# Making the split parts of queries and keys over 128 rows and moving them with transfers inside SBUF

## Chip, cores and metric

The kernel runs on one core of a Trainium2 chip. The metric is the device time of one execution in microseconds (us). The kernel before takes 1759.96 us, the median of 3 runs (1759.52 to 1761.84).

## What is computed

The input is one sequence of 512 rows with 1024 columns in float32. Four parts follow one another: a differential attention with a gated feed-forward net, a chunked attention with a relative-position bias and another such net, a block that mixes two other mechanisms, and a last feed-forward net. Only the two attentions matter here. Cut to the lines that the change touches:

```python
# differential attention, 8 heads, each with two maps m of 64 columns
q = apply_rope(q, cos, sin) * (A_HEAD_DIM ** -0.5)
k = apply_rope(k, cos, sin)
sc = einsum('bqhmd,bkhmd->bhmqk', q, k)          # chunk-causal mask, then softmax over k
a = p[:, :, 0] - lam * p[:, :, 1]
o = einsum('bhqk,bkhe->bqhe', a, v)
...
# chunked attention, 16 heads of 64 columns
sc = einsum('bnqhd,bnkhd->bhnqk', q, k_band) + bias
o = einsum('bhnqk,bnkhd->bnqhd', softmax(sc), v_band)
```

## The kernel before, in words

**Precision by parts.** TensorE multiplies in a reduced float32 form (F32R). To keep the precision, an operand w is split into a high part hi (a copy into F32R, on ScalarE) and a low part lo = w - hi (on VectorE), and a product is the sum of three: hi*hi, hi*lo, lo*hi (`passes`, L293 to L296). Weights come from HBM over the SP queue (`Weights.load`, L65), are split at L126 and L129, and are then used.

**Queries and keys.** A projection makes 128 rows by 512 columns, transposed: 64 rows for each of two maps of one head (differential attention) or for two heads (chunked attention). The product of scores for one of the two needs only 64 rows, so `stacked` (L556) stacks high and low parts to fill 128. For queries, tile `qk` 0 or 1 holds the high part in the map's own 64 rows and the low part in the other 64. For keys, `qk` 2 or 3 holds the high part in both halves, and `kl` the low part in both. Two products then give all four terms (`stacked_scores`, L580): L581 with the high keys, L582 with the low keys. `stacked` makes each 64-row piece by an instruction of its own: L569 copies the own high part, L571 makes the low part, for keys L573 copies the high part to the other rows and L578 (differential attention) or L575 (chunked, `twice=True`) makes the low part for the other rows. ScalarE and VectorE may write other rows than they read.

**Differential attention** (`attention_a`, L585). After a projection, `rope` (L621) turns the rows: four ScalarE copies (L626) into x[3], then three VectorE operations (L627 to L629) with a result in gb[:, 0]. Three steps of the projection stream later (`DELAY`), `rope_split` calls `stacked` on it. `scores` (L657) makes, for a block of 128 queries, the two maps' scores, their maxima (L670), exponentials with sums (L671, `accum_out`), a copy of the first map's sum into `sums[h]` (L677), and the combination (L676 to L680). `transposes` (L684) brings the result to the rows that `values_product` (L695) needs; `norm_sums` and `norm_apply` follow, with a power on POOL (L717).

**Chunked attention** (`attention_b`, L825). `split` calls `stacked` on the projection's bank in PSUM. `load_bias` (L833) loads 128 x 512 biases of one head through POOL's queue into one of `BB` = 3 buffers and then sets a corner with a POOL memset (L837). `scores` adds the bias with L873, which frees the buffer when its last block is done.

**Order.** `run_slots` (L343) goes through slots. Each slot has parts, four slots per head (`later(4 * h + n, scores, ...)`, transposes two slots later, and so on), and a stream of projection steps is paid out between them by a cost of 1.3 per step and a rate per slot: `A_RATE` = (3.4, 29, 2.0), `B_RATE` = (2.0, 54, 1.25). In the first attention the projection of a head completes some slots ahead of its first scores, in the second further ahead. Outside `manual_schedule` blocks (and but for SP, whose order is the program's everywhere) the Tile scheduler decides each engine's order when the program is built, from priorities, data and its own estimates of durations; on the chip each engine's queue runs in that fixed order. `qk` and `kl` have two buffers each, so the parts of a head wait for the scores of the head two before. The same two `qk` buffers take split weights at the end of an attention.

Of the kernel before, what the change touches and what calls it, by code (L numbers as in the profile page):

```python
# [10 lines left out]
F32 = mybir.dt.float32  # L11
F32R = mybir.dt.float32r
AF = mybir.ActivationFunctionType
OP = mybir.AluOpType
# [4 lines left out]
S, D = 512, 1024  # L19
NT = S // 128  # L20
# [14 lines left out]

DELAY = 3

BB = 3


WO2, AT = (4, 4, 0, 0), ((0, 4), (0, 4), (0, 2))
# [125 lines left out]
def body(ctx, tc, ins, out, stop=None, dbg=None):  # L167
    nc = tc.nc
# [78 lines left out]
    small = ctx.enter_context(tc.tile_pool(name="small", bufs=4))  # L247
# [7 lines left out]
    x = [const.tile([128, D], F32, name=f"x{t}") for t in range(NT)]  # L255
# [29 lines left out]
    gb = const.tile([128, 2, D], F32, name="gb")  # L285
# [12 lines left out]
    def bank(*shape):  # L298
        return psum.tile([128, *(shape or (512,))], F32, name="ps")
# [253 lines left out]
                stream += [(1.3, lambda g=n - 8, t=t, c=c: values(g, t, c)) for t in range(NT) for c in range(2)]  # L553
        return stream

    def stacked(pool, qk, j, which, p, scale=0.125, twice=False):  # L556

        if which == 0:
            both = pool.tile([128, 4 * S], F32, name="qk").bitcast(F32R)
            qk[j] = [both[:, n * S:n * S + S] for n in range(4)]
            kl = pool.tile([128, 2 * S], F32, name="kl").bitcast(F32R)
            qk[j] += [kl[:, :S], kl[:, S:]]
        part, rows, sc = qk[j], (slice(0, 64), slice(64, 128)), scale if which == 0 else 1.0
        for m in range(2):
            own, other, src, st = rows[m], rows[1 - m], p[rows[m]], part[2 * which + m]
            nc.scalar.activation(st[own], src, AF.Copy, scale=sc)  # L569
            lo = st[other] if which == 0 else part[4 + m][own]  # L570
            nc.vector.scalar_tensor_tensor(lo, src, sc, st[own].bitcast(F32), op0=OP.mult, op1=OP.subtract)  # L571
            if which == 1:
                nc.scalar.activation(st[other], src, AF.Copy)  # L573
                if twice:
                    nc.vector.scalar_tensor_tensor(part[4 + m][other], src, sc, st[own].bitcast(F32),  # L575
                                                   op0=OP.mult, op1=OP.subtract)
                else:
                    nc.scalar.activation(part[4 + m][other], lo.bitcast(F32), AF.Copy)  # L578

    def stacked_scores(p, part, m, i, N):  # L580
        yield lambda: nc.tensor.matmul(p[:, :N], part[m][:, ts(i)], part[2 + m][:, :N], start=True, stop=False)  # L581
        yield lambda: nc.tensor.matmul(p[:, :N], part[m][:, ts(i)], part[4 + m][:, :N], start=False, stop=True)  # L582


    def attention_a(es, oT, wo):  # L585
        pool = lambda name, bufs, **kw: es.enter_context(tc.tile_pool(name=name, bufs=bufs, **kw))
        persist, work = pool("a_const", 1), pool("a_work", 2)
# [3 lines left out]
        gcol, lam = cols_a[:, 0:1], cols_a[:, 4:8]  # L591
# [20 lines left out]
        qk, V, state, late = {}, {}, {}, []  # L612
# [17 lines left out]
            late.append([DELAY, rope_split, (h, which, r)])  # L630

        def rope_split(h, which, r):
            stacked(work, qk, h, which, r)

        def project(h, which, part):
            tick(1)
# [18 lines left out]
        soft, sums = {}, {}  # L655

        def scores(h, i, place):  # L657
            n = 128 * (i + 1)
            N = max(256, n)
            st = small.tile([128, 8], F32, name="a_st")  # L660

            e = x[(4 * h + place) % 3].rearrange("p (m k) -> p m k", m=2)
            ps = [bank(), bank()]
            for products in zip(*(stacked_scores(ps[m], qk[h], m, i, N) for m in range(2))):
                for product in products:
                    product()
            for m in range(2):
                p = ps[m]
                nc.vector.memset(p[0:64, n - 64:n], NEG)
                nc.vector.tensor_reduce(st[:, m:m + 1], p[:, :n], axis=AX.X, op=OP.max, negate=True)  # L670
                nc.scalar.activation(e[:, m, :n], p[:, :n], AF.Exp, bias=st[:, m:m + 1],  # L671
                                     accum_out=st[:, 2 + m:3 + m])

            if h not in sums:
                sums[h] = small.tile([128, NT], F32, name="a_s0")
            nc.vector.reciprocal(st[:, 4:5], st[:, 3:4])  # L676
            nc.vector.tensor_copy(sums[h][:, i:i + 1], st[:, 2:3])  # L677
            nc.vector.scalar_tensor_tensor(st[:, 5:6], st[:, 4:5], lam[:, 3:4], st[:, 2:3],
                                           op0=OP.mult, op1=OP.mult)
            nc.vector.scalar_tensor_tensor(e[:, 0, :n], e[:, 1, :n], st[:, 5:6], e[:, 0, :n],  # L680
                                           op0=OP.mult, op1=OP.add)
            soft[h, i] = e
# [142 lines left out]
    def attention_b(es, oT, wo, tails):  # L825
        pool = lambda name, bufs, **kw: es.enter_context(tc.tile_pool(name=name, bufs=bufs, **kw))
        persist, work = pool("b_const", 1), pool("b_work", 2)
        aT = tuple(persist.tile([128, 4, S], F32R, name=f"aT{q}") for q in "hl")
        for a in aT:
            nc.vector.memset(a[:, 3, 256:384].bitcast(F32), 0.0)  # L830
        qk, V, bias, soft, state, o_ = {}, {}, {}, {}, {}, {}

        def load_bias(hd):  # L833
            t = work.tile([128, S], F32, name="bias", bufs=BB)
# [3 lines left out]
            bias[hd] = t  # L838

        def split(j, which, p):  # L840
            stacked(work, qk, j, which, p, -0.125, True)

        def project(j, which, part):
            p = part_project(("bq" if which == 0 else "bk", j), state, part)
# [517 lines left out]
```

## Time and profile before

| what | value |
|---|---|
| time, median of 3 runs | 1759.96 us (1759.52 to 1761.84) |
| the profiled execution's own time | 1759.88 us |
| its span, first to last instruction | 1758.0 us |
| TensorE (PE) busy | 1727.9 us, 98% |
| VectorE (DVE) busy | 1184.7 us, 67% |
| ScalarE (ACT) busy | 875.1 us, 50% |
| GpSimd (POOL) busy | 70.9 us, 4% |
| granted TensorE clock, mean | 0.998 |
| differential attention | about 20 to 240 us |
| chunked attention | about 620 to 840 us |

The busy share is a mean over all stages. Matmuls are pipelined and their ends are modelled, so a busy TensorE need not be at its peak. Who waited for whom is inferred from semaphores; idle time of an engine that does not limit costs nothing by itself.

### The profile page before, as it was taken

The numbers are of one execution on the slowest core, as the hardware profiler recorded it, in microseconds if no ns is written. First come the engines' busy times: TensorE is split into PE (matmuls) and PEld (weight loads), VectorE is DVE, ScalarE is ACT, GpSimd is POOL, SyncE is SP. The second block draws the span as 40 slices with busy tenths as digits, with TensorE's granted clock in tenths as the row PEclk, the third lists the DMA queues.
The fourth block names the chain that finished last, engine by engine and source line by source line (L and its number), as shares of the span: only waits on it lengthen the run. The fifth ranks groups of instructions, "written<-read, shape, count | busy, mean of one in ns | idle before, by whom it ended". The sixth has DMA issues, their size and how long they took to land.

```text
span 1758.0 us, 26549 instructions
## 1 busy us (share of the span) xinstructions
PE 1727.9 (98%) x10496; PEld 1527.2 (87%) x10496; DVE 1184.7 (67%) x2028; ACT 875.1 (50%) x1470; POOL 70.9 (4%) x125
## 2 busy tenths in 40 slices
PE   8899999999999999999999999999999999999998
PEld 8688879999988888888899999888877899988886
DVE  6888856988844567767689888347546588763333
ACT  6878833444533258888344444333425445552221
POOL 0000002000000000000000000001001100000000
PEclk9999999999999999999999999999999999999999
DMA  6221226333443142322324244341322233443321
GB/s 206 61 61 61 83 97 206 108 110 107 120 132 120 48 120 79 97 78 73 108 78 118 84 131 139 102 121 49 109 73 91 72 86 96 128 124 108 97 96 48
DMA packets 198235, 176.83 MB, mean 101 GB/s; under 512 B 7008, under 2 KB 175136, under 8 KB 198112
## 3 DMA queue, kind: packets, MB, share of 16 engines
q1 hardware_dynamic: 194384, 162.48, 30.9%
q0 software_dynamic: 3152, 10.84, 2.1%
q8 instruction: 82, 1.34, 0.3%
q10 hardware_dynamic: 576, 1.84, 0.3%
q14 instruction: 41, 0.34, 0.1%
HBM read 172.99 MB, written 7.38 MB: 103 GB/s over the span
## 4 chain that ended last, share of the span: by engine, by line
PE 89%; ACT 6%; DVE 4%; issue 1%; DMA 0%; POOL 0%; SPq 0%; DVEq 0%; POOLq 0%; ACTq 0%
PE ps L296 52%; PE ps L382 30%; PE ps L896 1%; PE ps L312 1%; PE ps L884 1%; ACT whi L126 1%; ACT x L626 1%; PE ps L581 1%; PE ps L582 1%; ACT qk L573 1%; DVE wlo L129 1%; ACT qk L569 0%; PE ps L688 0%; ACT b_e L875 0%; PE ps L1096 0%
## 5 line engine op out<-in xcount | busy, mean ns | idle before, releaser
L126 ACT ACTIVATE whi<-wraw 128x1024 fp32r<-128x1024 f32 (+2 forms) x326 | 329.3, 1014 | 310.1 <-PE ps L296 183.7
L129 DVE TENSOR_TENSOR wlo<-wraw,whi 128x1024 fp32r<-128x1024 f32 (+2 forms) x326 | 379.9, 1168 | 133.9 <-ACT whi L126 132.2
L296 PE MATMUL ps<-xh,whi 128*128 128x256 f32 (+1 forms) x1260 | 406.6, 324 | 1.0 <-ACT xh L314 1.0
L296 PE MATMUL ps<-xl,whi 128*128 128x256 f32 (+1 forms) x1260 | 405.4, 322 | 0.5 <-DVE xl L315 0.3
L296 PE MATMUL ps<-xh,wlo 128*128 128x256 f32 (+1 forms) x1260 | 405.6, 322 | 0.0
L296 PEld LDWEIGHTS ps<-xh,whi 128*128 128x128 f32 x1260 | 238.5, 190 | 18.7 <-ACT xh L314 2.4
L296 PEld LDWEIGHTS ps<-xh,wlo 128*128 128x128 f32 x1260 | 239.4, 190 | 17.1
L296 PEld LDWEIGHTS ps<-xl,whi 128*128 128x128 f32 x1260 | 239.5, 190 | 16.9 <-DVE xl L315 1.0
L382 PE MATMUL ps<-whi,sh 128*128 128x512 f32 x568 | 175.9, 390 | 0.0
L382 PE MATMUL ps<-wlo,sh 128*128 128x512 f32 x568 | 175.5, 389 | 0.0
L382 PE MATMUL ps<-whi,sl 128*128 128x512 f32 x568 | 175.5, 389 | 0.0
L296 PE MATMUL ps<-th,whi 128*128 128x256 f32 x624 | 173.2, 277 | 0.0
L296 PE MATMUL ps<-tl,whi 128*128 128x256 f32 x624 | 172.8, 277 | 0.0
L296 PE MATMUL ps<-th,wlo 128*128 128x256 f32 x624 | 172.6, 277 | 0.0
L764 DVE TENSOR_TENSOR sl<-h,sh 128x512 fp32r<-128x512 f32 x76 | 52.1, 690 | 177.1 <-ACT sh L763 177.1
L763 ACT ACTIVATE sh<-h 128x512 fp32r<-128x512 f32 x76 | 46.7, 629 | 212.9 <-PE ps L382 204.1
L382 PEld LDWEIGHTS ps<-wlo,sh 128*128 128x128 f32 x568 | 106.6, 188 | 22.2
L382 PEld LDWEIGHTS ps<-whi,sl 128*128 128x128 f32 x568 | 106.6, 188 | 22.2
L382 PEld LDWEIGHTS ps<-whi,sh 128*128 128x128 f32 x568 | 106.3, 188 | 21.8
L296 PE MATMUL ps<-whi,xh 128*128 128x256 f32 (+1 forms) x384 | 125.1, 326 | 0.0
L296 PE MATMUL ps<-wlo,xh 128*128 128x256 f32 (+1 forms) x384 | 123.1, 321 | 0.0
L296 PE MATMUL ps<-whi,xl 128*128 128x256 f32 (+1 forms) x384 | 123.1, 321 | 0.0
(333 smaller groups left out, 2840.9 us busy)
## 6 DMA issues: line engine op xcount, KB each, us to landing
wraw<-in_ffn_w_in SPq DMA_DIRECT2D x76, 512.0 KB, 4.4
wraw<-in_w_ff SPq DMA_DIRECT2D x61, 512.0 KB, 4.0
wraw<-in_ffn_w_out SPq DMA_DIRECT2D x44, 512.0 KB, 3.6
wraw<-in_a_w_qkv SPq DMA_DIRECT2D x23, 512.0 KB, 3.9
wraw<-in_w_in SPq DMA_DIRECT2D x20, 512.0 KB, 3.8
wraw<-in_kv_w SPq DMA_DIRECT2D x16, 512.0 KB, 4.0
room<-in_ffn_w_in SPq DMA_DIRECT2D x12, 512.0 KB, 4.0
copies<-extd POOLq DMA_DIRECT2D x16, 320.0 KB, 8.2
```

What stands on the lines that cost most here:

```text
L126: self.nc.scalar.activation(hi[:, sl], t[:, sl], AF.Copy)
L129: self.nc.vector.tensor_tensor(lo[:, sl], t[:, sl], hi[:, sl].bitcast(F32), op=OP.subtract)
L296: nc.tensor.matmul(ps, lhs[a][lsel], rhs[b][rsel], start=first and n == 0, stop=last and n == 2)
L312: nc.tensor.transpose(p[:, k, :], y[:, ts(4 * c + k)], ident)
L382: nc.tensor.matmul(self.banks[t][c], act[a][:, ts(t)], w[b][:, 0, c * 512:(c + 1) * 512], start=first and n == 0, stop=last and n == 2)
L573: nc.scalar.activation(st[other], src, AF.Copy)
L581: yield lambda: nc.tensor.matmul(p[:, :N], part[m][:, ts(i)], part[2 + m][:, :N], start=True, stop=False)
L582: yield lambda: nc.tensor.matmul(p[:, :N], part[m][:, ts(i)], part[4 + m][:, :N], start=False, stop=True)
L626: nc.scalar.activation(qs[32 * g:32 * g + 32], p[32 * (g ^ 1):32 * (g ^ 1) + 32], AF.Copy)
L763: nc.scalar.activation(hi, src[k], AF.Copy)
L764: nc.vector.tensor_tensor(lo, src[k], hi.bitcast(F32), op=OP.subtract)
L884: nc.tensor.transpose(p[:, j], e[:, ts(j)], ident)
```

## The change

`stacked` gets two scratch tiles of 128 rows, `hi` and `lo`. One ScalarE copy makes the high part of all 128 rows and one VectorE operation the low part. Then transfers inside SBUF, issued on POOL's queue, bring 64 rows at a time to their places: four for queries, eight for keys. The variant `twice` is gone. In the differential attention the scratch is a half of x[3] (the rope's work rows) for hi and the rope's result itself for lo, a half each for queries and keys. In the chunked attention it is a half of gb[:, 0] and a new tile `low`, the same for queries and keys; `BB` goes from 3 to 2. In `scores` of the differential attention the exponential's sum of the first map goes straight into `sums[h]`, so the copy L677 is gone, and `sums[h]` is allocated ahead of the products.

```diff
-BB = 3
+BB = 2
...
-    def stacked(pool, qk, j, which, p, scale=0.125, twice=False):
+    def stacked(pool, qk, j, which, p, hi, lo, scale=0.125):
...
+        hi, lo, move = hi.bitcast(F32R), lo.bitcast(F32R), nc.gpsimd.dma_start
+        nc.scalar.activation(hi, p, AF.Copy, scale=sc)
+        nc.vector.scalar_tensor_tensor(lo, p, sc, hi.bitcast(F32), op0=OP.mult, op1=OP.subtract)
         for m in range(2):
-            own, other, src, st = rows[m], rows[1 - m], p[rows[m]], part[2 * which + m]
-            nc.scalar.activation(st[own], src, AF.Copy, scale=sc)
-            lo = st[other] if which == 0 else part[4 + m][own]
-            nc.vector.scalar_tensor_tensor(lo, src, sc, st[own].bitcast(F32), op0=OP.mult, op1=OP.subtract)
-            if which == 1:
-                nc.scalar.activation(st[other], src, AF.Copy)
-                if twice:
-                    nc.vector.scalar_tensor_tensor(part[4 + m][other], src, sc, st[own].bitcast(F32),
-                                                   op0=OP.mult, op1=OP.subtract)
-                else:
-                    nc.scalar.activation(part[4 + m][other], lo.bitcast(F32), AF.Copy)
+            own, other = rows[m], rows[1 - m]
+            if which == 0:
+                move(part[m][own], hi[own])
+                move(part[m][other], lo[own])
+            else:
+                for r in rows:
+                    move(part[2 + m][r], hi[own])
+                for r in rows:
+                    move(part[4 + m][r], lo[own])
...
-            stacked(work, qk, h, which, r)
+            stacked(work, qk, h, which, r, x[3][:, which * S:which * S + S], r)
...
+            if h not in sums:
+                sums[h] = small.tile([128, NT], F32, name="a_s0")
             for products in zip(*(stacked_scores(ps[m], qk[h], m, i, N) for m in range(2))):
...
                 nc.scalar.activation(e[:, m, :n], p[:, :n], AF.Exp, bias=st[:, m:m + 1],
-                                     accum_out=st[:, 2 + m:3 + m])
-
-            if h not in sums:
-                sums[h] = small.tile([128, NT], F32, name="a_s0")
+                                     accum_out=st[:, 3:4] if m else sums[h][:, i:i + 1])
             nc.vector.reciprocal(st[:, 4:5], st[:, 3:4])
-            nc.vector.tensor_copy(sums[h][:, i:i + 1], st[:, 2:3])
-            nc.vector.scalar_tensor_tensor(st[:, 5:6], st[:, 4:5], lam[:, 3:4], st[:, 2:3],
+            nc.vector.scalar_tensor_tensor(st[:, 5:6], st[:, 4:5], lam[:, 3:4], sums[h][:, i:i + 1],
...
+        low = persist.tile([128, S], F32, name="low")
...
-            stacked(work, qk, j, which, p, -0.125, True)
+            stacked(work, qk, j, which, p, gb[:, 0, S:], low, -0.125)
```

## Rows read from the trace of the kernel before

**Rows 1.** Stretches of both attentions: length, busy us (instructions), clock, DMA share, GB/s.
```profile
core 0: us, PE busy (x) PEld busy (x) DVE busy (x) ACT busy (x) POOL busy (x), PEclk, DMA share, GB/s
40.00:240.00 200.00, 188.10 (x1089) 161.30 (x1088) 162.41 (x420) 155.44 (x325) 8.58 (x8) 0.99 0.24 74
640.00:840.00 200.00, 197.26 (x1133) 167.72 (x1132) 144.88 (x363) 161.51 (x364) 8.89 (x26) 1.00 0.29 85
```
**Rows 2.** TensorE's waits in 40 to 245 us: total, times, longest.
```profile
PE ps L688 <- DVE a_s L677: 2.9, 1, 2.9
PE ps L296 <- ACT aTh L690: 2.1, 2, 1.7
PE ps L688 <- DVE x L680: 2.1, 1, 2.1
PE ps L581 <- ACT qk L573: 1.5, 2, 1.2
```
**Rows 3.** Stretches of 2 us behind the wait at 86 us; columns as in group 1.
```profile
86.00:88.00 2.00, 1.22 (x6) 1.25 (x7) 1.97 (x6) 1.95 (x4) 0.00 (x0) 0.62 0.00 0
88.00:90.00 2.00, 2.00 (x11) 2.00 (x11) 1.94 (x4) 1.97 (x4) 0.00 (x0) 0.52 0.00 0
```
**Rows 4.** Instructions that write tile qk: ns min/median/max, first and last start.
```profile
L569 ACT ACTIVATE qk<-gb x32: 615/628/635, 29.7 to 201.9; 64x512 fp32r<-64x512 f32 x32
...
L569 ACT ACTIVATE qk<-ps x32: 573/592/596, 633.6 to 795.8; 64x512 fp32r<-64x512 f32 x32
L571 DVE SCALAR_TENSOR_TENSOR qk<-gb,qk x16: 685/686/689, 32.1 to 193.3; 64x512 fp32r<-64x512 f32 x16
L573 ACT ACTIVATE qk<-gb x16: 628/630/632, 32.8 to 203.2; 64x512 fp32r<-64x512 f32 x16
...
L573 ACT ACTIVATE qk<-ps x16: 574/589/597, 640.1 to 797.6; 64x512 fp32r<-64x512 f32 x16
```
**Rows 5.** Instructions that write tile kl.
```profile
L571 DVE SCALAR_TENSOR_TENSOR kl<-gb,qk x16: 673/686/690, 34.0 to 202.6; 64x512 fp32r<-64x512 f32 x16
L578 ACT ACTIVATE kl<-kl x16: 615/629/632, 34.8 to 204.4; 64x512 fp32r<-64x512 f32 x16
L571 DVE SCALAR_TENSOR_TENSOR kl<-ps,qk x16: 664/689/695, 638.5 to 796.4; 64x512 fp32r<-64x512 f32 x16
L575 DVE SCALAR_TENSOR_TENSOR kl<-ps,qk x16: 683/689/694, 641.4 to 798.4; 64x512 fp32r<-64x512 f32 x16
```
**Rows 6.** Lines L677 and L706.
```profile
L677 DVE COPY a_s<-a_st x32: 132/144/156, 41.9 to 224.4; 128x1 f32<-128x1 f32 x32
...
L706 ACT ACTIVATE gb<-a_o x8: 629/632/635, 77.8 to 232.2; 128x512 f32<-128x512 f32 x8
```
**Rows 7.** Tile bias: issue (ns), its engine's idle time (us, times), landing.
```profile
L835 POOL DMA_DIRECT2D bias<-copies x16: 536/536/612, 615.9 to 803.8; - x16
...
  DVE b_st L873: 62.9, 7
  DMA bias<-copies: 41.7, 16
...
DMA to landing us min/median/max: 2.8/3.3/6.1
```
**Rows 8.** DMA issues by line: KB each, median us to landing.
```profile
extd<-gb POOLq DMA_DIRECT2D x1, 15.9 KB, 1.6
```
**Rows 9.** Timeline of POOL, near 280 us: start, us, line, operation.
```profile
279.79 4.16 POOL L822 DMA_DIRECT2D copies<-extd  x8 [1.68 <-DMA extd<-gb]
```
**Rows 10.** Pieces of the chain of waits in order of time: start us, us, what.
```profile
55.32 0.60 DVE gb L629
...
60.14 0.64 ACT kl L578
...
132.04 0.63 ACT kl L578
...
179.10 0.61 DVE gb L629
...
184.74 0.63 ACT kl L578
```
**Rows 11.** Timeline of VectorE at 128 us.
```profile
127.91 0.68 DVE L629 TENSOR_TENSOR gb<-gb,x 128x512 f32<-128x512 f32 x1
```

## The prediction, made before the changed kernel ran

> **What bounds the kernel now.** I read the busy shares first, then the two attention stages by stretches, then who TensorE waits for, and last the pieces of the chain of waits. TensorE is busy for 98% of the span, so the change, which takes no product away, can give back only time in which TensorE stands still. In the differential attention (40 to 240 us) TensorE is busy for 188.1 of 200 us beside ScalarE's 155 and VectorE's 162; in the chunked attention (640 to 840 us) for 197.3 of 200 [rows 1]. That leaves 11.9 and 2.7 us, a floor, since the ends of matmuls are modelled. What the reader is to see in the waits is that none is for a weight load: transposes, value products and scores wait for ScalarE and VectorE, whose queues run late [rows 2]. One such wait costs twice: after the 2.9 us one TensorE ran at a granted clock of 0.62 and then 0.52 for four microseconds, its 1.2 GHz level [rows 3]. Of its busy 1.22 and 2.00 us there, 0.38 and 0.48 are lost, 1.4 us in all. So the most that can come back is about 11.9 + 2.7 + 1.4 = 16 us.
>
> The profiled execution took 1759.88 us with a span of 1758.0; the median of the runs shown is 1759.96, the same within 0.1. I work from 1759.9.
>
> **What is removed.** In the first attention, per head, two ScalarE copies for the queries and six for the keys, and two VectorE subtractions for each: 32 x 0.628 + 16 x 0.630 [rows 4] + 16 x 0.629 [rows 5] = 40.2 us of ScalarE, and 32 x 0.686 = 22.0 us of VectorE [rows 4, 5]. In the second, 32 x 0.592 + 16 x 0.589 = 28.4 us of ScalarE [rows 4], and 32 of L571 and 16 of L575 at 0.689 = 33.1 us of VectorE [rows 5]. The copy of sums is 32 x 0.144 = 4.6 us of VectorE [rows 6]. The order of `sums[h]` before the products is no instruction; it costs nothing.
>
> **What is added.** Per stage 16 copies and 16 subtractions over 128 rows. A copy of twice the rows takes no longer: the 128x512 one from SBUF took 0.632 us [rows 6], the 128x512 VectorE operation 0.68 [rows 11]. So ScalarE pays back 16 x 0.63 = 10.1 us in the first stage and 16 x 0.59 = 9.4 in the second, VectorE 16 x 0.69 = 11.0 in each. Net: first stage ScalarE -30.1, VectorE -15.6 us (19% and 10% of their busy time); second stage -19.0 and -22.1 (12% and 15%).
>
> Then 12 transfers per head or pair, 96 per stage, of 64 rows x 2 KB = 128 KB, all on POOL's queue. An issue there took 0.536 us [rows 7], and eight went out back to back in 4.16 us [rows 9], so 12 are 6.4 us of a queue that does almost nothing else: per stage 51 of 200 us beside 9. The bytes are 96 x 0.128 = 12.6 MB in 200 us, 63 GB/s more beside 74 and 85, at a DMA share of 0.24 and 0.29 [rows 1]; even doubled it is not full, and no weight is waited for, so I put the loads at nothing. If that cover were gone, a weight's split would wait on ScalarE, and TensorE for it.
>
> **The unknown: how long a transfer takes to land.** No row shows one from SBUF to SBUF. Below stands 1.6 us for 15.9 KB [rows 8], above 6.1 us, the worst of the 256 KB bias loads, three of which went out together; their median was 3.3 [rows 7]. I take 3.3, since half the bytes is offset by eight in a row. The keys are complete 0.63 (the high part) + 8 x 0.54 (the issues; the subtraction runs beside the first two) + 3.3 = 8.2 us after the rope's last addition; with the two ends 6.6 and 11.0. Today it takes from the end of L629 to the end of the last L578: 60.8 - 55.9 = 4.9 us, 132.7 - 128.6 = 4.1 and 185.4 - 179.7 = 5.7 [rows 10, 11]; a fourth head near 200 us has 4.9. So the keys become later by 3.3, 4.1, 2.5 and 3.3 us.
>
> **Where later keys matter.** By the slots and rates the projection stream leaves heads 0, 2, 3 and 5 most of a slot or more (a slot is 5 to 6 us) between the split and the first score, and heads 1, 4, 6 and 7 (the four above) next to nothing: TensorE already waits there for L573 [rows 2]. In the second stage the stream is ahead by three slots or more from the second pair on; only the first pair is tight.
>
> **What the path gets.** First stage: the 2.9 us wait at 86 us hangs on a norm chain behind ScalarE's L569 and L573; it loses some 2 us and the 1.4 of the clock, 3.4 together. The 2.1 us for x (L680, near 139 us) comes after six key copies, 3.9 us of ScalarE that shrink to 0.6: all 2.1. The 2.1 us for L690 hangs on one copy and four rope copies: 1.2. The smaller ones, half of 3: 1.5. Sum 8.2 us. The waits for L573 stay, as waits for a transfer. Second stage: 1.2 of 2.7, its waits being softmax latencies that only a shorter queue helps. New waits: between nothing and 13.2 us (the four heads' whole delay). The scheduler places the scores by its own estimate of the transfers and fills TensorE from the projection stream, so I take the low side, 2.0 us, the first pair of the second stage included. The sum is -8.2 - 1.2 + 2.0 = -7.4: **1752.5 us**.
>
> What moves to POOL brings its waits along. A bias load there waits for the last score of an earlier head (62.9 us over seven), and the memset behind each load waits for its landing (41.7 us over 16) [rows 7]; transfers queued behind these wait too, 3 us or so. `BB = 2` moves the load from two heads ahead to one; four slots of some 3 us cover 0.5 + 3.3 + 0.1 us: nothing, unless twelve issues stand ahead of it (6.4 us), and then it still arrives. The scratch rows (x[3], gb, low) are written again a projection later, 5 slots of the stream, 7 us: just after 8.2 us of transfers begin to clear, so ScalarE could be held for a microsecond; in the range.
>
> A POOL issue beside busy VectorE shows no lengthening here: minimum and median are both 0.536 us, with VectorE 72% busy [rows 1, 7]. The Trainium skill, "SBUF — State Buffer", section "SBUF: two separate sides", warns of the contrary: descriptors of a transfer issued from GpSimd are held while VectorE runs certain copies through both ports. By that rule every issue could wait out one VectorE instruction; by the row none does.
>
> **Rivals.**
> - *The tight heads wait in full (slower).* If the order on TensorE stays as today, the four heads' scores stand at the front for 13.2 us instead of 2.0, and two of the waits of over 3 us lower the clock again (1.4 each, about 3): 1752.5 + 11 + 3 = 1766. It decides once the transfers land more than about 2 us later than the scores are placed. For it: TensorE waits at this place now. Against it: a planner that sees the transfers. 0.16.
> - *POOL's issues stretch.* Each of eight issues held for one VectorE instruction of 0.69 us makes the keys 5.5 us later; on four heads, with half of it filled by other products, +11 and 3 of clock: 1767. The 16 issues at 0.536 us speak against it. It is the rule of the Trainium skill named above. 0.03.
> - *A draw.* Half of the 8.2 comes back, because the chains behind the waits (softmax, rope's four copies) are untouched, and the new waits take 4: 1759.9 - 4.1 - 0.6 + 4 = 1759. 0.18.
> - *Nearly all idle time goes.* ScalarE at 125 of 200 us catches up, and the new waits are filled: -14 of the 16: 1746. 0.13.
> - *The forecast*: 0.50, its own range 1747 to 1757. That the copies or subtractions would not be halved is excluded by the code.
>
> **Numbers.** About 0.2%, 3.5 us, can be told from no change. Faster takes 0.13 + most of 0.50: 0.60; within 0.2% the draw's larger part and the forecast's end: 0.17; slower 0.23. The range 1744 to 1765 takes in all but the far ends of the slow cases.
>
> **What would show it.** Right: L569 to L578 gone from ScalarE, 32 operations of 0.63 and 0.69 in their place; TensorE idle in 40 to 240 us down from 11.9 to about 6; no wait for VectorE near 86 and 139 us, no clock below 0.9 there; POOL busy some 60 us per stage, landings near 3 us. Wrong: L581 waiting for transfers on heads 1, 4, 6 and 7 with several microseconds each; ScalarE waiting for transfers before L626 or the high part; POOL's queue filled by waits; new idle time of TensorE elsewhere from another order.

## The result, and the profile after

The changed kernel took 1782.24 us (median of 4 runs, 1777.99 to 1783.17) beside 1760.39 of the kernel before on the same chip: ratio 1.0118, 95% interval 1.0102 to 1.0134. It is 21.9 us slower; the forecast was 7.4 faster. The profiled execution took 1783.17 us with a span of 1781.4, against 1758.0 before: 23.4 us to be found.

First where they lie. Three marks of the trace cut the span: the last product of the output weights with tile oT of the first attention, the first copy of a high part in the second, and the last output-weight product there.

```
us                                    before    after   difference
start to last oT product, first       267.5     275.0    +7.5
from there to the second attention    366.1     366.2    +0.1
first copy to last oT product, second 231.8     242.5   +10.7
from there to the end                 892.6     897.7    +5.1
```

Each attention lost, although ScalarE and VectorE got their relief. The stretches of [rows 1], after the change (length, busy us and instructions of PE, PEld, DVE, ACT, POOL, granted clock, DMA share, GB/s):

```profile
40.00:240.00 200.00, 183.11 (x1053) 157.89 (x1053) 147.13 (x371) 129.56 (x282) 50.38 (x91) 0.97 0.52 125
640.00:840.00 200.00, 188.94 (x1098) 162.66 (x1098) 114.98 (x302) 135.45 (x303) 59.04 (x124) 0.98 0.66 149
```

ScalarE is down from 155 and 162 to 130 and 135 us, and TensorE stands still for 16.9 and 11.1 us where it did for 11.9 and 2.7. The DMA share has doubled. The lines that replaced [rows 4, 5], first attention and then second (busy, mean ns of one, idle time of the engine before them and what ended it):

```profile
L569 ACT ACTIVATE x<-gb 128x512 fp32r<-128x512 f32 x16 | 10.1, 629 | 12.3 <-DVE gb L631 11.0 <-DVE a_st L678 1.2
L570 DVE SCALAR_TENSOR_TENSOR gb<-gb,x 128x512 fp32r<-128x512 f32 x16 | 10.8, 678 | 0.4 <-ACT x L569 0.3
...
L569 ACT ACTIVATE gb<-ps 128x512 fp32r<-128x512 f32 x16 | 9.5, 591 | 10.9 <-DMA qk<-gb 10.8
L570 DVE SCALAR_TENSOR_TENSOR low<-ps,gb 128x512 fp32r<-128x512 f32 x16 | 11.0, 686 | 17.8 <-DMA qk<-low 11.1 <-DMA kl<-low 3.8 <-ACT gb L569 2.9
```

The durations are those forecast. What is new is at the end of the lower two: in the second attention both engines wait for transfers before they may write the scratch rows again.

TensorE's waits in 40 to 245 us answer to [rows 2] (total, times, longest):

```profile
PE ps L584 <- DMA kl<-gb: 8.5, 4, 4.1
PE ps L583 <- DMA qk<-x: 3.9, 2, 3.1
PE ps L583 <- DMA kl<-gb: 2.7, 2, 1.4
PE ps L689 <- DVE x L681: 1.2, 2, 1.0
```

The waits at 86 and near 139 us for the softmax chain are gone but for 1.2 us, and so is the clock's fall of [rows 3] (1.00 from 86 to 90 us). In their place stand 15.1 us of waits for transfers, at heads 0, 1, 4 and 6. Two of them bring the clock down in their turn: after 2.5 us at head 0 it stood at 0.67 and 0.50 from 46 to 50 us, and at head 6, after waits of 3.1 and 4.1 us, it was back at 1.2 GHz until near 197 us. Stretches of 2 us at head 6, columns as above:

```profile
186.00:188.00 2.00, 0.00 (x0) 0.00 (x0) 1.83 (x3) 0.04 (x1) 0.63 (x2) 0.66 1.04 148
188.00:190.00 2.00, 0.00 (x0) 0.00 (x0) 0.00 (x0) 0.58 (x1) 0.51 (x1) 0.50 1.13 309
190.00:192.00 2.00, 1.11 (x2) 0.63 (x3) 1.05 (x3) 0.00 (x0) 0.06 (x1) 0.50 0.68 129
```

TensorE did nothing for four microseconds and came back at 0.50, its 1.2 GHz level. In the second attention the same view (630 to 890 us) names a wait of 4.5 us for a transfer, at the first scores, one more of 0.5 us, and softmax waits, which have grown. After the change, then before it:

```profile
PE ps L583 <- DMA qk<-gb: 4.5, 1, 4.5
PE ps L886 <- ACT gb L879: 3.9, 4, 1.5
PE ps L886 <- ACT b_e L879: 2.2, 3, 1.5
```
```profile
PE ps L884 <- ACT b_e L877: 1.1, 3, 0.7
PE ps L884 <- ACT gb L877: 0.5, 3, 0.2
```

The transfers into tile kl, first and second attention (issue: ns min/median/max, first and last; then issue to landing, us):

```profile
L580 POOL DMA_DIRECT2D kl<-gb x32: 509/542/578, 35.8 to 214.0; - x32
DMA to landing us min/median/max: 2.5/3.4/7.2
...
L580 POOL DMA_DIRECT2D kl<-low x32: 509/537/569, 650.6 to 818.4; - x32
DMA to landing us min/median/max: 2.2/5.0/8.3
```

The issue is as forecast (0.536), the landing 3.4 us in the middle of the first attention, but 5.0 in that of the second, and 7.2 and 8.3 at worst. Last, the end: the instructions of the kernel's last line on POOL's queue, before and after.

```profile
L1358 POOLq DRAIN  x3: 51/98/4175, 1752.3 to 1757.8; - x3
```
```profile
L1360 POOLq DRAIN  x3: 51/97/9973, 1770.6 to 1781.1; - x3
```

Before the program ends, POOL's queue is drained; that took 4.2 us and now 10.0, while SP and the compute engines stand finished. This is the +5.1: of the 5.8 us that the drain grew by, the rest passed while the last output was still on its way.

### The profile page after: what moved, and what is told of

The parts are those of the page before. It is cut to its first block, busy times and chain, and to the rows that moved or that the text cites. A ratio compares the mean times of both kernels' runs of the same rounds, so it can differ in the third digit from the quotient of the medians.

```text
span 1781.4 us, 26859 instructions
## 1 busy us (share of the span) xinstructions
PE 1732.6 (97%) x10496; PEld 1531.9 (86%) x10496; DVE 1145.6 (64%) x1948; ACT 829.8 (47%) x1390; POOL 169.4 (10%) x317
## 4 chain that ended last, share of the span: by engine, by line
PE 54%; DMA 2%; issue 1%; DVE 1%; ACT 1%; POOL 0%; DVEq 0%; POOLq 0%; ACTq 0%
PE ps L296 30%; PE ps L382 21%; DMA qk<-low 1%; PE ps L898 1%; PE ps L886 1%; PE ps L312 0%; PE ps L1098 0%; DMA qk<-gb 0%; PE ps L1103 0%; PE ps L583 0%; DMA kl<-low 0%; PE ps L584 0%; DVE wlo L129 0%; PE ps L1062 0%; PE ps L1116 0%
## 5 line engine op out<-in xcount | busy, mean ns | idle before, releaser
L382 PEld LDWEIGHTS ps<-whi,sh 128*128 128x128 f32 x568 | 106.3, 188 | 21.7
```

Of the source, the lines that this page charges most:

```text
L382: nc.tensor.matmul(self.banks[t][c], act[a][:, ts(t)], w[b][:, 0, c * 512:(c + 1) * 512], start=first and n == 0, stop=last and n == 2)
```

## The experiments

The theory (T): the transfers take more than the relief gives, by their landing in front of the scores, by the scratch rows that they hold, and by POOL's closing drain. Rivals: another order of TensorE's products (O); a relief worth nothing (L). Thirteen more kernels ran. In the table, "first" and "second" are the two attentions by the marks above, "rest" the stretch to the end, and the count is of the transfers that POOL issues in the whole program.

```
                              median  ratio to before, interval   first  second  rest   POOL count, drain
before                        1760.4  1                           267.5  231.8   892.6   43   4.17
changed                       1782.2  1.0118 (1.0102 to 1.0134)   275.0  242.5   897.7  235   9.97
transfers left out            1742.7  0.9901 (0.9887 to 0.9915)   253.9  228.2   892.8   43   4.17
new way in first alone        1766.4  1.0037 (1.0025 to 1.0048)   271.3  231.8   892.8  139   2.13
new way in second alone       1774.1  1.0081 (1.0068 to 1.0095)   268.1  243.3   892.4  139   2.13
before, 192 idle transfers    1769.6  1.0053 (1.0039 to 1.0067)   271.9  231.8   898.0  235   9.97
DELAY = 1                     1778.7  1.0105 (1.0090 to 1.0120)   268.8  244.6   897.7  235   9.97
transfers on SP               1760.6  1.0000 (0.9990 to 1.0009)   262.6  238.8   893.0   43   4.17
own halves direct             1759.6  0.9997 (0.9987 to 1.0006)   260.7  235.3   897.1  107   9.40
tight heads the old way       1762.8  1.0015 (1.0005 to 1.0024)   264.6  238.2   892.3  163   4.09
own halves, SP                1757.9  0.9984 (0.9976 to 0.9993)   262.7  235.8   892.8   43   4.17
own halves, SP, pair 0 old    1751.8  0.9953 (0.9940 to 0.9967)   260.3  230.6   892.5   43   4.17
own halves, 32 idle more      1755.4  0.9971 (0.9960 to 0.9983)   260.9  234.2   892.4  139   2.13
before, sums edit alone       1761.8  1.0006 (0.9997 to 1.0015)   269.5  231.8   892.6   43   4.17
tight old, B queries old      1754.2  0.9962 (0.9949 to 0.9976)   263.5  230.2   892.3  135   1.81
```

The stage lengths are of one profiled execution each; runs of one kernel differ by up to 6.5 us (the changed one's by 5.2), so differences of 1 or 2 us between rows are not read as effects.

### Transfers left out

```diff
-        nc.scalar.activation(hi, p, AF.Copy, scale=sc)
-        nc.vector.scalar_tensor_tensor(lo, p, sc, hi.bitcast(F32), op0=OP.mult, op1=OP.subtract)
-        for m in range(2):
-...
+        nc.scalar.activation(part[2 * which], p, AF.Copy, scale=sc)
+        nc.vector.scalar_tensor_tensor(part[4 if which else 1], p, sc, part[2 * which].bitcast(F32),
+                                       op0=OP.mult, op1=OP.subtract)
...
-        yield lambda: nc.tensor.matmul(p[:, :N], part[m][:, ts(i)], part[2 + m][:, :N], start=True, stop=False)
-        yield lambda: nc.tensor.matmul(p[:, :N], part[m][:, ts(i)], part[4 + m][:, :N], start=False, stop=True)
+        yield lambda: nc.tensor.matmul(p[:, :N], part[m][:, ts(i)], part[2][:, :N], start=True, stop=False)
+        yield lambda: nc.tensor.matmul(p[:, :N], part[m][:, ts(i)], part[4][:, :N], start=False, stop=True)
```

> The changed kernel with its 192 transfers left out: the high and the low part are written once over 128 rows, straight into the tiles that the score products read, so the two halves are not brought to their rows (the scores are therefore not those of the reference), and scratch rows are not used. Theory T (the transfers are the loss: their landing at the tight heads, the scratch rows they hold, and POOL's closing drain): with them gone the relief stands alone, about 1745 to 1757 us, below the kernel before; the waits for POOL's tiles qk and kl before the scores vanish, and the closing drain is back from 10.0 to about 4.2 us. Rival O (another order on TensorE and new softmax waits make the loss, with or without transfers): 1765 us or more. Rival L (transfers cost, but the relief is worth nothing): 1758 to 1762.

1742.65 us, a little below the range of T: the relief alone is worth 17.9 us, and the transfers cost 1782.24 - 1742.65 = 39.6. O and L fall. In this kernel both maps of a head read the same two key tiles; the number and the shapes of the products are as before. TensorE's stretches and its only waits of 40 to 245 us that are left:

```profile
40.00:240.00 200.00, 198.03 (x1151) 172.12 (x1150) 157.89 (x395) 132.73 (x291) 9.63 (x10) 1.00 0.26 81
640.00:840.00 200.00, 199.82 (x1146) 170.87 (x1145) 126.06 (x340) 140.31 (x326) 10.48 (x29) 1.00 0.27 81
```
```profile
PE ps L296 <- ACT aTh L680: 0.9, 1, 0.9
PE ps L713 <- POOL a_r L707: 0.6, 1, 0.6
PE ps L382 <- DVE oTl L717: 0.2, 1, 0.2
PE ps L678 <- DVE x L670: 0.2, 1, 0.2
```

Idle time falls from 11.9 to 2.0 and from 2.7 to 0.2 us. By the table the relief is 13.6 us in the first attention and 3.6 in the second; the transfers then take 21.1, 14.3 and 4.9 us in the two attentions and at the end.

### One attention at a time

The first edit is that of the new way in the first attention alone (with three bias buffers and without low), the second that of the second alone.
```diff
-            stacked(work, qk, j, which, p, gb[:, 0, S:], low, -0.125)
+            stacked_old(work, qk, j, which, p, -0.125, True)
...
-            stacked(work, qk, h, which, r, x[3][:, which * S:which * S + S], r)
+            stacked_old(work, qk, h, which, r)
```

> The new way in the first (differential) attention alone; the second goes as in the kernel before (three bias buffers, no extra scratch). By the matmul-by-matmul comparison of the two traces the first attention lost 7.5 us, the second 10.8 and the end 5.1 (96 of 192 issues would be 2.6 of it). Theory T, losses add up stage by stage: 1760.4 + 7.5 + 2.6 = about 1770.5 (1768 to 1773). Rival: the second stage's loss comes from what the first left (shifted order, DMA): then 1778 or more. Rival: the first stage's loss is an accident of its order that goes with the other stage's code: 1763 or less.

> The new way in the second (chunked) attention alone, with two bias buffers; the first goes by the four partial copies and subtractions of before (without the copy of sums). Theory T, losses add up: 1760.4 + 10.8 + 2.6 = about 1774 (1771 to 1776), ScalarE and VectorE held by the two scratch rows for some 10 us each as in the changed kernel. Rival (second stage only suffers after a late first one): 1766 or less.

1766.38, below the range of T, and 1774.11, within it. The losses add, though roughly: +5.8 and +13.5 make 19.3, and with the long drain's 5.1, which neither of the two kernels has, 24.4 beside +21.9 together. Neither attention suffers from the other (231.8 and 268.1, as before). The share of the drain that was expected at half the transfers, 2.6 us, did not come: at 139 issues the drain is shorter than before.

```profile
L1383 POOLq DRAIN  x3: 98/198/2133, 1756.2 to 1761.6; - x3
```

### The drain by itself

```diff
+    def idle_transfers():
+        spare = dram.tile([192, 64, 128], F32, name="spare")
+        for n in range(192):
+            nc.gpsimd.dma_start(spare[n], ident[0:64])
...
-    ffn(0, [*after_attention[:3], [lambda: T(3), bias_rows]], layer_norm, T)
+    ffn(0, [*after_attention[:3], [lambda: T(3), bias_rows, idle_transfers]], layer_norm, T)
```

> The kernel before, with 192 further transfers of 32 KB (64 rows x 512 bytes, from an SBUF constant to a spare array in DRAM that nothing reads) issued on POOL's queue in the first feed-forward stage, far from both attentions. Theory D (the closing drain on POOL grows with the number of transfers POOL has issued, some 30 ns each): the last drain lasts about 10 us instead of 4.2 and the time is about 1760.4 + 5 = 1765 to 1766, with nothing lost in the attentions. Rival (the longer closing drain was late transfers or late work of the changed kernel): the drain stays at 4.2 us and the time within 1759 to 1762.

1769.62, more than expected. The drain came as D has it, to the nanosecond that of the changed kernel, though these transfers carry a quarter of the bytes and are long done:

```profile
L1363 POOLq DRAIN  x3: 51/93/9973, 1757.0 to 1767.5; - x3
```

The other 4.4 us are a misplacement: the planner issued the 192 at the start of the program instead of in the feed-forward stage, and the first attention's norm chain, which has one step on POOL, came late: TensorE waited 3.9 us for it, beside 0.6 before.

```profile
PE ps L723 <- POOL a_r L717: 3.9, 2, 3.4
```

### Parts sooner, and another queue

```diff
-DELAY = 3
+DELAY = 1
```

> The changed kernel with DELAY = 1 instead of 3: the high and low parts of the first attention are written two units of the stream sooner after the rope, so the transfers start sooner; nothing else differs. Theory T (at the tight heads 0, 1, 4, 6, 7 TensorE stands waiting for the landing, 20 us with the clock's fall): parts that come 2 to 4 us sooner take about half of it back, 1770 to 1776 us. Rival O (the planner places the scores just as much sooner, or ScalarE's queue does not allow the copy sooner): within 1779 to 1785.

1778.70, between the two ranges. The first attention did gain, 275.0 to 268.8, with the waits put down to transfers into kl down from 11.2 to 6.1 us and those into qk up from 3.9 to 5.1; the second, in which nothing was edited, came out 2.1 longer, which is no more than the spread of executions.

```diff
-        hi, lo, move = hi.bitcast(F32R), lo.bitcast(F32R), nc.gpsimd.dma_start
+        hi, lo = hi.bitcast(F32R), lo.bitcast(F32R)
+        move = lambda out, src: nc.sync.dma_start(out.bitcast(F32), src.bitcast(F32))
```

> The changed kernel with its 192 transfers issued on SP's queue instead of POOL's. Theory Q (what costs is POOL's part: eight issues of 0.52 us one behind another, its waits behind bias loads and memsets, and the closing drain of 10 us): the drain falls back by some 5 us, the landings come sooner, 1765 to 1775. Rival L (landing itself and the waits for scratch rows cost, on any queue): 1776 to 1779, only the drain given back. Rival W (a transfer's wait on SP holds the weight loads behind it, and TensorE waits for weights): 1785 or more.

1760.57, below every range: the same 192 transfers of the same bytes cost 21.7 us less on SP's queue; of the spans' 20.9, 12.4 lie in the first attention, 3.7 in the second and 4.7 at the end. Q is right and was put too small; W fell. The tile kl in the first attention:

```profile
L569 SPq DMA_DIRECT2D kl<-gb x32: 461/594/1326, 38.4 to 202.1; - x32
...
DMA to landing us min/median/max: 2.2/2.4/3.1
```

The issue is slower than POOL's, so a row of eight takes a little longer to send; but none lands later than 3.1 us, against 7.2. Why, two heads of the changed kernel show. Head 3, near 98 us, and head 4, near 132 us, and with head 4 a load of weights (512 KB) that SP issued at 132.7:

```profile
L580 POOL DMA_DIRECT2D kl<-gb x4: 517/536/547, 97.9 to 99.9; - x4
...
DMA to landing us min/median/max: 2.9/3.0/3.1
```
```profile
L580 POOL DMA_DIRECT2D kl<-gb x4: 519/540/559, 131.6 to 134.1; - x4
...
DMA to landing us min/median/max: 2.7/5.9/6.9
```
```profile
L80 SPq DMA_DIRECT2D wraw<-in_a_w_qkv x1: 368/368/368, 132.7 to 132.7; - x1
...
DMA to landing us min/median/max: 7.0/7.0/7.0
```

Transfers and weights lengthen one another: 3.0 becomes 6.9, and the load takes 7.0 where before the median was 3.9. So it goes by heads: a weight load was issued among the eight at heads 0, 1, 4 and 6, and the eighth landed 5.5 to 6.9 us after its issue; at heads 2, 3 and 7 none was until at least 1 us after the last, and it took 3.0 to 3.4. Head 5 lies between, at 4.3 with no load beside it; why stays open. How busy VectorE was does not tell the two kinds apart: 88% of the time at head 7, with 3.4 us, and 61% at head 6, with 6.1. The loads were not moved by themselves in any run, so this is read from eight heads and from the other queue. On SP's queue the load goes out behind the transfers. SP's timeline at the same head:

```profile
125.40 1.10 SPq L569 DMA_DIRECT2D qk<-x  x2
126.60 1.19 SPq L569 DMA_DIRECT2D kl<-gb  x2
127.83 1.23 SPq L569 DMA_DIRECT2D qk<-x  x2
129.10 1.24 SPq L569 DMA_DIRECT2D kl<-gb  x2
130.44 0.53 SPq L80 DMA_DIRECT2D wraw<-in_a_w_qkv  x1
```

All eight landed within 2.4 us, the load behind them within 3.9. The Trainium skill, "DMA: Bandwidth & Descriptors", says in its sections "Issuing engines are not separate DMA queues" and "Queues, rings and completion order" that all issuing engines share the same 16 DMA engines, which take turns between queues and take up the work of one queue in order. The trace agrees on both counts: beside each other, 6.9 and 7.0 us; one behind the other, 2.4 and 3.9.

The order can also go against the transfers. In the second attention SP sent a weight load 0.4 us ahead of the keys' eight near 725 and near 775 us, and they took 3.5 to 5.9 us to land; near 748 us, with no load issued for 3.9 us before, 2.2 to 2.4. That attention kept 7.0 of its 10.7 us on SP's queue, and the wait at its first scores stayed (4.6 us).

### Only the halves that have to move

```diff
         for m in range(2):
             own, other, src, st = rows[m], rows[1 - m], p[rows[m]], part[2 * which + m]
             nc.scalar.activation(st[own], src, AF.Copy, scale=sc)
             lo = st[other] if which == 0 else part[4 + m][own]
             nc.vector.scalar_tensor_tensor(lo, src, sc, st[own].bitcast(F32), op0=OP.mult, op1=OP.subtract)
             if which == 1:
...
+                nc.gpsimd.dma_start(st[other], st[own])
+                nc.gpsimd.dma_start(part[4 + m][other], lo)
```

> The kernel with the sums edit in which queries are made as before (a copy and a subtraction per half), the keys' own halves are written straight to their rows by one copy and one subtraction each, and only the other halves (4 of 64 rows per head, 64 transfers in all) are brought over by POOL; no scratch rows, three bias buffers. It removes 4 ScalarE copies per head in the first attention and 2 copies and 2 subtractions per pair in the second. Theory T (the loss goes with the number of transfers in a row, the scratch rows and the lateness of the last landing): keys are complete about 1.3 + 0.5 to 1.5 + 3.3 = 5 to 6 us after the rope, near today's 4 to 6, so the relief wins: 1750 to 1758, with no longer drain. Rival L (one landing in the keys' chain costs as much as eight, 3 to 5 us at each of five or six tight places): 1762 to 1772.

1759.61, in neither range, with the cause plain: the attentions take 260.7 and 235.3, which would make some 1755, but the 107 issues fell on a long drain.

```profile
L1354 POOLq DRAIN  x3: 51/98/9402, 1749.1 to 1759.0; - x3
```

So the next pair: the same with its transfers on SP's queue, and the same on POOL with 32 transfers more that nobody reads (as above, 32 in place of 192). The edit shown is that of the first:

```diff
-                nc.gpsimd.dma_start(st[other], st[own])
-                nc.gpsimd.dma_start(part[4 + m][other], lo)
+                nc.sync.dma_start(st[other].bitcast(F32), st[own].bitcast(F32))
+                nc.sync.dma_start(part[4 + m][other].bitcast(F32), lo.bitcast(F32))
```

> The kernel with own halves written straight (as in the run with 64 transfers on POOL, 1759.6 us), its 64 transfers issued on SP's queue instead. Theory T (the loss is landings that share the DMA engines with a 512 KB weight load, and POOL's closing drain, which at that run's 107 issues lasted 9.4 us): drain back to 4.2 us (-5.2), the weight load queues behind the transfers instead of beside them, and the wait of 4.0 us before the second attention's first scores shrinks: 1750 to 1755 us. Rival (SP's own waits hold weight loads, or landings are no shorter): 1757 to 1762.

> The kernel with own halves written straight and 64 transfers on POOL (1759.6 us), plus 32 transfers of 32 KB that nothing reads, from an SBUF constant to a spare array, so that POOL issues 139 transfers instead of 107. So far the closing drain lasted 4.17 us at 43 issues, 9.40 at 107, 2.13 at 139, 4.09 at 163, 9.97 at 235, whatever the transfers carry. Theory D (the drain depends on the count alone, and not in one direction): at 139 it lasts 2.1 us, and more work makes the kernel faster, by about 5 us: 1753 to 1757, unless the early issues delay the first attention as 192 did (by 4). Rival (the drain follows what is late at the end, or the bytes): 9.4 us or more, 1759 to 1765.

With 32 more, 1755.35, as D said: the drain is 2.13 us, and more work made the kernel 4.3 us faster.

```profile
L1359 POOLq DRAIN  x3: 51/98/2133, 1748.2 to 1753.3; - x3
```

On SP, 1757.91, in the rival's range and not in T's: the drain is back at 4.17 and the stretch to the end at 892.8, but the attentions take 262.7 and 235.8, no less than on POOL. With four transfers a head the queue makes no difference there that these runs can tell. At the second attention's first scores a wait of 4.0 us on POOL is one of 3.4 on SP. That should go with pair 0 in the old way:

```diff
+            if j == 0:
+                stacked_old(work, qk, j, which, p, -0.125, True)
+            else:
+                stacked(work, qk, j, which, p, -0.125)
```

> The same, with pair 0 of the second attention made in the old way (no transfer in the key chain where the stream leaves no slack). Theory T: what is left of the wait at the second attention's first scores goes, another 1 to 4 us: 1747 to 1753. Rival (that wait is only moved to the next pair): the same as the run without this edit, within 1 us.

1751.78, ratio 0.9953 (0.9940 to 0.9967), in the range of T: 8.9 us less than the kernel before. That is 6.1 us less than without this edit, more than the 1 to 4 expected of it; of the spans' 8.2, 5.2 lie in the second attention. Its stretches:

```profile
40.00:240.00 200.00, 193.13 (x1123) 166.68 (x1122) 163.15 (x401) 141.20 (x304) 8.45 (x8) 1.00 0.35 100
640.00:840.00 200.00, 198.66 (x1139) 169.13 (x1139) 135.75 (x355) 151.62 (x350) 9.34 (x27) 1.00 0.37 102
```

TensorE stands still for 6.9 and 1.3 us, about halfway between the kernel before and the one without transfers.

### The tight heads, and the scratch rows

```diff
-            stacked(work, qk, h, which, r, x[3][:, which * S:which * S + S], r)
+            if h in (0, 1, 4, 6, 7):
+                stacked_old(work, qk, h, which, r)
+            else:
+                stacked(work, qk, h, which, r, x[3][:, which * S:which * S + S], r)
...
+            if j == 0:
+                stacked_old(work, qk, j, which, p, -0.125, True)
+            else:
...
```

> The changed kernel in which heads 0, 1, 4, 6 and 7 of the first attention and pair 0 of the second are made in the old way (four partial copies and subtractions, no transfers), the rest in the new: 120 transfers instead of 192. Theory T (the loss of the first attention sits at the tight heads alone): the first attention is no longer than before, perhaps 2 to 4 us shorter from the relief of the three other heads; in the second the wait of 5 us at pair 0 goes, the holds on the single scratch rows stay: 1760 to 1766. Rival (the transfers cost wherever they are, by DMA load or the order): 1772 or more.

1762.78, as T has it. The first attention is 2.9 us shorter than before, and no wait of TensorE for a transfer is left there, so its loss sat at the tight heads. In the second the wait at pair 0 goes (242.5 to 238.2), but 6.4 us more than before stay. What holds them: VectorE's and ScalarE's waits for transfers in 640 to 840 us, and TensorE's for the softmax.

```profile
DVE low L570 <- DMA qk<-low: 7.9, 3, 3.5
DVE low L570 <- DMA kl<-low: 2.7, 1, 2.7
ACT gb L569 <- DMA qk<-gb: 6.4, 7, 2.1
```
```profile
PE ps L916 <- ACT b_e L909: 3.9, 4, 1.5
PE ps L916 <- ACT gb L909: 3.5, 3, 1.8
```

Whether the scratch rows or the landings beside weights do this was still open. The last run takes the queries off the scratch rows and leaves the keys' eight transfers:

```diff
-            if j == 0:
+            if j == 0 or which == 0:
                 stacked_old(work, qk, j, which, p, -0.125, True)
```

> The run with the tight heads made the old way (1762.8 us; first attention: heads 2, 3, 5 new, second: pairs 1 to 7 new), but with the queries of all pairs of the second attention made the old way too, straight to their rows. Each scratch row is then written once per pair instead of twice 7 us apart, and 8 transfers per pair are left of 12. Theory S (the second attention loses by the scratch rows: the subtraction and the copy of the next projection wait for the transfers of the last one, and the softmax work queued behind them comes late): the waits of VectorE for low and of ScalarE for gb vanish, the second attention shrinks from 238.2 (first split to last product with the output weights) to about 231, near the kernel before's 231.8; with a closing drain of some 2 us at 135 issues, 1754 to 1758 us. Rival C (it loses by landings beside weight loads, and eight keys' transfers are enough): 235 or more, 1760 or more.

1754.23, as S has it. The second attention takes 230.2 us, 8.0 less; no wait for low or gb is left, the keys' transfers land about as late as before (medians 4.1 us into qk and 3.7 into kl, beside 3.3 and 4.3), and TensorE's softmax waits of 640 to 840 us are down from 7.4 to 1.0:

```profile
PE ps L916 <- ACT b_e L909: 0.7, 1, 0.7
PE ps L916 <- ACT gb L909: 0.3, 2, 0.2
```

So the scratch rows are the likelier cause, and landings that nobody waits for cost nothing to be seen. The two are not wholly apart, since four transfers a pair went too.

The sums edit, alone in the kernel before (the three lines of the change in `scores`):

> The kernel before with the copy of sums left out and nothing else. 32 VectorE copies of 0.144 us, 4.6 us of an engine that is busy 72% of the stage. Theory: beside other work, nothing to 2 us comes back, 1758 to 1760. Rival: the copy stands in the softmax chain that TensorE waits for, 32 times some 0.1 us: 1756 to 1757.5.

1761.75, ratio 1.0006 (0.9997 to 1.0015), above both ranges: worth nothing that can be measured. The relief comes from the copies and subtractions of queries and keys.

## Why the prediction was wrong

```
term of the sum, us               forecast   measured   from
relief, first attention             -8.2      -13.6     transfers left out
relief, second attention            -1.2       -3.6     transfers left out
new waits, first                 \  +2.0      +21.1     changed against transfers left out
new waits, second                /            +14.3     the same; 4.3 at pair 0, 8.0 with the queries' transfers
end of the program                   0         +4.9     POOL's drain
sum                                 -7.4      +23.1     of spans; 23.4 measured directly
```

**Removed and added work: right.** The new copies took 0.629 and 0.591 us and the subtractions 0.678 and 0.686, as costed; over the whole kernel ScalarE lost 45.3 us of busy time (875.1 to 829.8) and VectorE 39.1, against 49.1 and 37.7 in the steps. POOL's 50 and 59 us in the two stretches answer to the forecast 60. That none of this was on the path in full, only where TensorE waits, was right too; the relief was put too small. Even the 16 us that were to be the most are less than the 17.9 measured. Without transfers nearly all idle time goes, which the prediction had as a rival (-14) at 0.13: with ScalarE's queue shorter by about a seventh (132.7 us for 155.4) the chains behind it, which were thought untouched, came in time as well.

**The step that failed is the new waits**: bounded by 0 and 13.2 us and then taken at 2.0, because "The scheduler places the scores by its own estimate of the transfers and fills TensorE from the projection stream". It does not fill it. TensorE waits 15.1 us for transfers in the first attention, and after two of the waits it runs at its 1.2 GHz level. The upper bound fell as well, and by a named term: landing at 3.3, with the loads of the other queue "at nothing". The keys were forecast complete 8.2 us after the rope, with 11.0 as the end of the range. That stretch, from the start of the high copy to the last landing, is 7.6 to 8.7 us at heads 2, 3, 5 and 7, and 12.2, 10.0, 11.3 and 11.0 at heads 0, 1, 4 and 6, where TensorE waits. The middle landing was right in this attention, 3.4 us, and useless: a landing is long where a weight load runs beside it, and it was long at four heads of eight, the waiting ones. The prediction asked whether the DMA engines would be full over 200 us (share 0.24, doubled), not what else is in flight in the 8 us that count.

Of the heads, 1, 4 and 6 were named. That TensorE "already waits there for L573" was read too widely: both waits of [rows 2] lie at head 6, between 180 and 184 us. After the change head 7 shows no wait for a transfer, and head 0, which was given slack, one of 2.5 us.

**The scratch rows** were to cost little: "so ScalarE could be held for a microsecond". In the second attention they held VectorE for 14.9 us and ScalarE for 10.8, and the softmax work queued behind the waiting instructions is what TensorE then waited for. The prediction saw that a row is written again 5 slots later, "just after 8.2 us of transfers begin to clear", and still priced it for one engine and without what stands behind it in the queue. That only the first pair is tight was right (4.3 us), and no engine but POOL is seen to wait for a bias tile; the last run on the scratch rows keeps `BB = 2` with a second attention of 230.2 us, 1.6 less than before, so two buffers showed no cost of their own.

**The drain** was in no step. POOL's queue was costed for its issues and its waits, not for the end of the program, where it took 4.9 us.

**The rivals.** "The tight heads wait in full", at 0.16 and 1766, is the mechanism of the first attention, with two falls of the clock as it said; its size was short by the collisions, and neither the second attention's scratch rows nor the drain were in it. The result lies 17 us above the range's end. "POOL's issues stretch" is not seen: 509 to 578 ns for the issues into kl, beside 536 before [rows 7]. The Trainium skill, "SBUF — State Buffer", section "SBUF: two separate sides", warns that they are held while VectorE runs certain copies; no such hold shows here, and how much of VectorE's work is of that kind no run tells. What stretched was not the issue but the landing, at the heads with a weight load beside it.

## What to carry to other kernels

A transfer that takes the place of a copy is priced by its last landing where the consumer waits, and that landing by what shares the DMA engines in those microseconds: look at which weight loads are due there, and put the urgent transfer ahead of them in the same queue rather than beside them in another. Here the move to SP's queue gave back 12.4 us in the first attention with twelve transfers a head, and nothing to be seen with four. Move only what must change rows and write the rest in place: 60 transfers without scratch rows, and none at the tight first pair, kept about half of the relief; 192 with scratch rows lost all of it and more than as much again. A single scratch buffer that DMA reads from is a wait of the next writer, and of all that is queued behind that writer on its engine.

## What the runs showed of the hardware that was not expected

POOL's closing drain depends on how many transfers POOL has issued, and on nothing else that was varied: 4.17 us at 43, 9.40 at 107, 1.81 at 135, 2.13 at 139, 4.09 at 163, 9.97 at 235. The same count gave the same drain in different kernels (2.13 in three of them, 9.97 in three). Bytes do not count (9.97 for 128 KB and for 32 KB each), nor when they were issued. Within a stretch it grows by 0.08 us per transfer ((9.40 - 4.17) / 64, (9.97 - 2.13) / 96), and between 107 and 135 it starts anew (near 113 if it starts from nothing with that slope, an estimate). What sets the step no run shows. Up to some 4 us it is hidden behind the transfers of the last output: the stretch to the end takes 892.3 us with a drain of 1.81 and 892.6 with 4.17. Above, it is the end of the program.

The two queues are not alike in landing: in the first attention, with no weight load issued until 0.7 us or more after the last, the eighth of a row of eight landed after 3.0 to 4.3 us from POOL (heads 2, 3, 5 and 7) and 2.4 from SP, though the first took 2.2 to 2.4 on both.
